# Splitting the output projection's weights early: as extra jobs of the first SwiGLU, kept in DRAM until the attention

## The chip, the cores and the metric

The kernel runs on one core of a Trainium2 chip. The metric is the device time of one execution in microseconds, as the median of several runs. A profile of one execution gives the start, the length and the wait of every instruction on the five engines: TensorE (PE in the profile, its weight loads PEld), VectorE (DVE), ScalarE (ACT), GpSimd (POOL) and SyncE (SP, which here only issues the DMAs).

## The reference, cut to what matters

One transformer block over 1024 tokens of width 1024, in float32:

```python
x = x + 0.5 * swiglu(rms_norm(x, ffn1_norm), ffn1_w_in, ffn1_w_out)      # D_FF = 2816
proj = rms_norm(x, mix_norm) @ w_mix_in                                   # q, k, v, gates
o_a = banded_attention(q_a, k_a, v_a, tbl[:, :8], 128, sinks_a)           # 8 heads, window 128
o_cmp, o_sel = nsa_cmp_sel(q_b, k_c, v_c, k_s, v_s, tbl_b)                # 8 heads, compressed and selected keys
o_win = banded_attention(q_b, k_w, v_w, tbl_b, 512, None)                 # the same 8 heads, window 512
o_b = gates[:, :, 0] * o_cmp + gates[:, :, 1] * o_sel + gates[:, :, 2] * o_win
x = x + concat([o_a, o_b]) @ w_mix_out                                    # the output projection, 1024 x 1024
x = x + 0.5 * swiglu(rms_norm(x, ffn2_norm), ffn2_w_in, ffn2_w_out)
```

## The kernel before, in words

**Arithmetic.** A float32 operand is split in two parts of type fp32r, a high part `h` (the operand rounded) and a low part `l` (what is left). A product is then three matmuls, `h*h + h*l + l*h` (`mm3`, lines 250 to 252). So every weight tile of 128 x 512 that comes from DRAM costs, beside its DMA, one pass that makes `whi` and one subtraction that makes `wlo`.

**Stages.** (1) The first SwiGLU's input stage (`first_stage`) multiplies the normed tokens with `ffn1_w_in`. It uses a Strassen-like scheme of seven products in place of eight for each of 20 pairs of column blocks `n`, so it subtracts weights from each other (line 806) and splits the results on ACT (line 458) and DVE (line 463); on POOL it multiplies gate and up (line 876). Beside this main work it runs *side jobs*: the sums and differences of `ffn1_w_out` that the next stage needs, four loads, four DVE subtractions and four stores to DRAM each (`sums_of`, line 783). A side job works in four fixed buffers: the second halves of the token tiles `X[2]` and `X[3]`, which are free at that time, and two buffers `side`. There are 12 of them, and they follow each other as soon as their buffers come free. (2) `second_stage` multiplies with `ffn1_w_out`. (3) Five chunks of `w_mix_in` make queries, keys, values and gates; the last chunk is called CH1. (4) The attention, in two halves `g` = 0 and 1 of the heads. In each half come eight query tiles `i`, and for each of them three parts A, sel and win: query-key products into PSUM (`lg`, line 1748), a DVE pass that adds the bias and takes the maximum (line 1787), the exponential on ACT (line 1795), its scaling on POOL (line 1811), transposes on PE (`ptr`, line 1923) that ACT and DVE copy out as a high and a low part (`ph` line 1931, `pl` line 1933), the products with the values (`pvo`, lines 1942 and 1943), and a finish on ACT and POOL (lines 1968, 1975, 1981, 1983). After win of tile `i` the output projection of this half follows: four pieces of six matmuls into `mo` (`make_out`), with the eight weight tiles of `w_mix_out` that belong to this half. (5) The second SwiGLU, with both of its stages.

**The weights of the output projection before.** The 16 tiles of 128 x 512 (`MO`, eight for each half) are *converted* in the attention by `conv`: a DMA into one of four buffers `wraw` (line 83), the high part on POOL (`Units.high`, line 88), the low part on DVE (`Units.low`, line 93). The pair `whi`/`wlo` takes one of nine slots. The same nine slots hold the eight tiles of CH1 before, and the scores of the first three attention parts.

**The order of the work.** All instructions are first listed as tasks, each with an engine, an estimated length, a wished position, dependencies and the buffers that it takes. A small planner (`Plan.run`) picks at each step the task that can start earliest by those estimates, and this fixes the program order of every engine. The order is worked out anew when a task is added or removed. On the chip every engine runs its list strictly in that order and waits at an instruction until its inputs are there; SP does the same with the DMAs that it issues, and a DMA also waits until the eighth DMA before it has finished. There are two plans: the first ends with stage 2, and the second holds everything from stage 3 to the end.

Of the kernel before, what the change touches and what calls it, by code (L numbers as in the profile page):

```python
# [9 lines left out]
F32R = mybir.dt.float32r  # L10
BF16 = mybir.dt.bfloat16
I32 = mybir.dt.int32
AF = mybir.ActivationFunctionType
# [7 lines left out]
D = 1024  # L21
KD = 8
FF = 2816
NF = 22
# [15 lines left out]
LATE = 4.5  # L40
# [17 lines left out]
class Units:  # L58
# [7 lines left out]
    def add(self, width, parts):  # L66
        self.units.append((width, parts))
        return len(self.units) - 1
# [120 lines left out]
def block_kernel(  # L189
# [37 lines left out]
    dr = pool("dr", space=DRAM)  # L227
# [26 lines left out]
    def dma(dst, src):  # L254
        if src.dtype == F32R:
            dst, src = dst.bitcast(F32), src.bitcast(F32)
        return nc.sync.dma_start(dst, src)
# [192 lines left out]
    def split(b, dep, src_users, pos, eng, pair=ws.pair, slots=None, chain=None, low="D"):  # L450
# [15 lines left out]
        return w, low, us  # L466

    def acc_ring(turns=("lg", "lg", "lg", "pv", "mo")):
        tile_no[0] += 1
        tag = turns[tile_no[0] % len(turns)]  # L470
        return tag, {"lg": r_lg, "pv": r_pv, "mo": r_mo}[tag]
# [138 lines left out]
    NK = NF // 2  # L610
# [4 lines left out]
    XS = [dr.tile([128, D], F32, name=f"xs{t}") for t in range(NT)]  # L615

    def in_src(w_in, n, j, part):
        return dram_ap(w_in, 512 * j * 2 * FF + part * FF + n * 128, [[4 * 2 * FF, 128], [2 * FF, 4], [1, 128]])
# [8 lines left out]

    def first_stage(layer, w_in, w_out, opn, scaled, units_, side, pos, weigh, at0, pieces, opened, xa=(), raws=None, gain=None, side_free=(), plain=2, begin=False):

# [161 lines left out]
        def weights_of(k):  # L791

            return [lambda j=j, c=c: dram_ap(w_out, (2 * k + j) * 128 * D + c * 512, [[D, 128], [1, 512]])
                    for j in range(2) for c in range(2)]
        SUB, ADD = OP.subtract, OP.add
        T_OPS = (("T1", "T3", "T2", "T4"), TS, ((0, 1, 0, SUB), (1, 3, 1, SUB), (3, 3, 0, SUB), (2, 2, 3, SUB)))
        S_OPS = (("S1", "S3", "S2", "S4"), AS, ((3, 2, 3, ADD), (2, 0, 2, SUB), (0, 3, 0, SUB), (1, 1, 0, SUB)))

        def less(a, b, at, deps):
# [3 lines left out]
            def emit():  # L803
# [10 lines left out]
                                          [stored[0, a] for a in ("A11", "A12", "A21", "A22")], *S_OPS))  # L814
        every = (NF - plain) / (len(jobs) + 0.5)
        half_done = {}
        for n in range(plain, NF):
            while jobs and n - plain >= every * (NK + 1 - len(jobs)):
                side_us = jobs.pop(0)(at)
# [235 lines left out]
    def s2_place():  # L1055
# [3 lines left out]
                                         lambda: side1, 2.0, "G", [],   # L1059
                                              [(0, 256), (256, 512)], none, raws=raws1, gain=lambda c: gcol[:, c], begin=s2_place)  # L1060

# [839 lines left out]
    pvo, mixes, outs = {}, {}, {}  # L1901
    chain = {"pv": None, "mo": None}

    def make_tiles(s):
# [10 lines left out]
        for j, (c, vt) in enumerate(tiles):  # L1915
# [4 lines left out]
            def flip4(c=c, st=st):  # L1920
                p = st["p"] = bank("a", name="ptr")
                for h in range(4):
                    PE.transpose(p[:, h * 128:(h + 1) * 128], s.P[h][:, c:c + 128], ident)  # L1923
            t = add("P", 0.43, pos, flip4, deps=[s.compressed] if vt is None else ready,
                    after=[opened], takes=[(r_a, a_users)])
            s.P_users.append(t)

            def high(st=st):
                st["ph"] = ring(p_kv, "ph", [128, 512], F32R, NPH)
                st["pl"] = ring(p_kv, "pl", [128, 512], F32R, NPH)  # L1930
                ACT.activation(st["ph"], st["p"], AF.Copy)  # L1931
            hi = add("A", 0.48, pos + 0.1, high, deps=[t], takes=[(r_ph, ph_users)])
            lo = add("D", 0.6, pos + 0.2, lambda st=st: DVE.tensor_tensor(  # L1933
# [56 lines left out]
    def make_out(s, parts):  # L1990
        g, i = s.g, s.i
        pos = s.pos + s.nt + 20.0
        for h in range(2):
            box, us, ms = {}, [], []
            for j in range(2):
# [3 lines left out]
                def piece(j=j, h=h, st=st, us_=us_, box=box):  # L1999
                    if j == 0:  # L2000
                        box["o"] = bank("mo")
                    for kk in range(2):
                        wh, wl = ws.out[us_[kk]]
                        mm3(box["o"], st["mh"][:, kk], st["ml"][:, kk], wh, wl, j == 0 and kk == 0, j == 1 and kk == 1)
# [19 lines left out]
    for u, pos in mo_convs:  # L2024
        conv(u, pos, [s.begin for s in subs[:EARLY]])
    for s in subs:
# [92 lines left out]
```

## Time and profile before

| what | us |
|---|---|
| median of 3 runs (lowest, highest) | 1912.22 (1911.73, 1912.34) |
| the profiled execution: its time / its span | 1910.23 / 1908.5 |
| PE busy | 1874.3 (98%) |
| DVE busy | 1373.8 (72%) |
| ACT busy | 920.8 (48%) |
| POOL busy | 428.6 (22%) |

By stage (the stretches are cut by hand at the stages' edges):

| stretch, us | stage | PE | DVE | ACT | POOL | DMA share |
|---|---|---|---|---|---|---|
| 0 to 450 | first SwiGLU, input | 447.0 | 334.2 | 184.6 | 89.0 | 0.51 |
| 450 to 635 | first SwiGLU, output | 185.0 | 110.9 | 84.2 | 0.6 | 0.77 |
| 635 to 880 | projections | 243.8 | 168.2 | 97.7 | 38.6 | 0.41 |
| 880 to 1258 | attention | 354.1 | 328.5 | 304.8 | 225.4 | 0.18 |
| 1258 to 1700 | second SwiGLU, input | 439.6 | 323.9 | 170.2 | 75.1 | 0.49 |
| 1700 to 1908.5 | second SwiGLU, output | 204.7 | 108.1 | 79.4 | 0.0 | 0.64 |

In a row of a timeline stand the start, the length, the engine, the line, the operation with output and inputs, and in brackets the idle time before it with what ended it. In a row of a view by windows stand, for each engine, the busy time and the number of instructions, then the granted TensorE clock, the busy share of the 16 DMA engines and GB/s. "PE 98% busy" counts a matmul that runs at a lower granted clock as busy too.

### The profile page before, as it was taken

Reading aid. Unit: us, or ns where it says so; the run is one execution under the profiler, and the core shown is the slowest. Engines: PE = TensorE matmul, PEld = TensorE weight load, DVE = VectorE, ACT = ScalarE, POOL = GpSimd, SP = SyncE. Lnnn points to the kernel's source line nnn. Section 1 sums busy time; section 2 is a strip of 40 time slices with the busy share of each in tenths; the row PEclk is TensorE's granted clock in tenths of the full one; section 3 lists DMA queues with packets and bytes.
Section 4 is the critical chain, followed back from the end, with each engine's and each line's share of the span. In section 5 each row is a group of like instructions: output and inputs, shape, how many; then the busy total and the mean of one; then the engine's idle time right before and its main releaser. Section 6 shows DMA issues by size and latency. Waiting matters only on the chain.

```text
span 1908.5 us, 27998 instructions
## 1 busy us (share of the span) xinstructions
PE 1874.3 (98%) x9094; PEld 1565.7 (82%) x9094; DVE 1373.8 (72%) x3120; ACT 920.8 (48%) x1951; POOL 428.6 (22%) x568
## 2 busy tenths in 40 slices
PE   9999999999999999998999899999999999999999
PEld 8888888888888889886788788777888888888887
DVE  7978776655755778467988888879788766655553
ACT  6433333333544444346877887854333333344442
POOL 5111111110000112015655764541111111110000
PEclk9999999999999999999999999999999999999999
DMA  5467742327886246244102311023677523368662
GB/s 171 145 225 256 236 153 89 128 97 278 295 252 199 83 118 180 67 141 156 51 23 60 104 61 56 24 66 127 225 232 239 183 92 101 120 238 303 195 214 99
DMA packets 244211, 290.25 MB, mean 152 GB/s; under 512 B 25424, under 2 KB 139488, under 8 KB 244064
## 3 DMA queue, kind: packets, MB, share of 16 engines
q1 hardware_dynamic: 244064, 288.46, 46.4%
q8 instruction: 72, 1.18, 0.3%
q14 instruction: 75, 0.61, 0.1%
HBM read 201.20 MB, written 90.33 MB: 153 GB/s over the span
## 4 chain that ended last, share of the span: by engine, by line
PE 92%; DVE 2%; ACT 2%; POOL 1%; issue 1%; DMA 1%; SPq 0%; DVEq 0%; ACTq 0%
PE lg L250 13%; PE lg L252 13%; PE lg L251 13%; PE mo L250 6%; PE mo L252 6%; PE mo L251 6%; PE pv L250 4%; PE pv L252 4%; PE pv L251 4%; PE ptr L1923 3%; PE a L252 3%; PE a L250 3%; PE a L251 3%; PE pvo L1943 2%; PE lg L1748 2%; PE pvo L1942 2%
## 5 line engine op out<-in xcount | busy, mean ns | idle before, releaser
L876 POOL TENSOR_TENSOR x<-x,x 128x512 f32<-128x512 f32 x80 | 117.6, 1471 | 679.3 <-DVE x L872 640.7
L463 DVE TENSOR_TENSOR wlo<-wraw,whi 128x512 fp32r<-128x512 f32 x286 | 204.3, 719 | 69.2 <-ACT whi L458 68.0
L458 ACT ACTIVATE whi<-wraw 128x512 fp32r<-128x512 f32 x274 | 170.1, 622 | 97.8 <-PE lg L251 46.6
L463 DVE TENSOR_TENSOR gpl<-graw,gph 128x512 fp32r<-128x512 f32 x154 | 106.9, 698 | 124.4 <-ACT gph L458 124.3
L458 ACT ACTIVATE gph<-graw 128x512 fp32r<-128x512 f32 x154 | 96.2, 630 | 195.4 <-PE pv L251 88.5
L868 ACT ACTIVATE x<-lg 128x512 f32<-128x512 f32 x96 | 57.4, 598 | 157.1 <-PE lg L252 157.1
L1933 DVE TENSOR_TENSOR pl<-ptr,ph 128x512 fp32r<-128x512 f32 x178 | 116.4, 684 | 18.3 <-ACT ph L1931 17.1
L1931 ACT ACTIVATE ph<-ptr 128x512 fp32r<-128x512 f32 x178 | 98.5, 595 | 31.1 <-PE ptr L1923 29.4
L88 POOL TENSOR_SCALAR whi<-wraw 128x512 fp32r<-128x512 f32 (+1 forms) x52 | 36.0, 696 | 316.9 <-PE mo L252 209.2
L458 ACT ACTIVATE whi<-x 128x512 fp32r<-128x512 f32 x108 | 67.4, 627 | 81.6 <-PE lg L251 41.6
L250 PE MATMUL a<-whi,gph 128*128 128x512 f32 x264 | 103.1, 391 | 0.0
L252 PE MATMUL a<-whi,gpl 128*128 128x512 f32 x264 | 102.8, 389 | 0.0
L251 PE MATMUL a<-wlo,gph 128*128 128x512 f32 x264 | 102.7, 389 | 0.0
L463 DVE TENSOR_TENSOR wlo<-x,whi 128x512 fp32r<-128x512 f32 x108 | 73.7, 685 | 31.3 <-ACT whi L458 31.1
L250 PE MATMUL lg<-xn0h,whi 128*128 128x512 f32 x232 | 90.7, 391 | 0.0
L252 PE MATMUL lg<-xn0h,wlo 128*128 128x512 f32 x232 | 90.3, 389 | 0.0
L251 PE MATMUL lg<-xn0l,whi 128*128 128x512 f32 x232 | 90.3, 389 | 0.0
L872 DVE TENSOR_TENSOR x<-lg,x 128x512 f32<-128x512 f32 x72 | 49.7, 690 | 54.2 <-PE lg L252 53.9
L252 PE MATMUL lg<-whi,gpl 128*128 128x512 f32 x198 | 77.1, 389 | 0.0
L250 PE MATMUL lg<-whi,gph 128*128 128x512 f32 x198 | 77.0, 389 | 0.0
L251 PE MATMUL lg<-wlo,gph 128*128 128x512 f32 x198 | 77.0, 389 | 0.0
L1811 POOL TENSOR_SCALAR Psel<-Psel,sc,gates 128x256 f32<-128x256 f32 (+7 forms) x60 | 52.1, 871 | 46.1 <-DVE sc L1803 19.8
(523 smaller groups left out, 5698.5 us busy)
## 6 DMA issues: line engine op xcount, KB each, us to landing
wraw<-in_ffn_w_in_dram SPq DMA_DIRECT2D x172, 256.0 KB, 3.3
wraw<-in_ffn_w_out_dram SPq DMA_DIRECT2D x66, 256.0 KB, 3.4
x<-in_ffn_w_out_dram SPq DMA_DIRECT2D x44, 256.0 KB, 4.0
qd<-qst SPq DMA_DIRECT2D x32, 256.0 KB, 2.1
xn0l<-qd SPq DMA_DIRECT2D x32, 256.0 KB, 2.7
wraw<-in_w_mix_in_dram SPq DMA_DIRECT2D x28, 256.0 KB, 2.8
x<-in_x_dram SPq DMA_DIRECT2D x12, 512.0 KB, 6.9
side<-in_ffn_w_out_dram SPq DMA_DIRECT2D x22, 256.0 KB, 4.8
```

Of the source, the lines that this page charges most:

```text
L250: PE.matmul(o, ah, bh, start=first, stop=False, **kw)
L251: PE.matmul(o, ah, bl, start=False, stop=False, **kw)
L252: PE.matmul(o, al, bh, start=False, stop=last, **kw)
L458: ACT.activation(w["h"], b["r"], AF.Copy)
L463: low = add(low, 0.69 if low == "D" else 1.25, pos + 0.5, lambda e=DVE if low == "D" else POOL: e.tensor_tensor(w["l"], b["r"], w["h"].bit ...
L868: ACT.activation(b["r"], o["o"], act)
L872: return add("D", 0.69, at, lambda b=tb[k], o=bx[o]: DVE.tensor_tensor(b["r"], o["o"], b["r"], op=OP.add), deps=deps)
L876: return add("G", 1.25, at, lambda a=tb[a], b=tb[b]: POOL.tensor_tensor(a["r"], a["r"], b["r"], op=OP.mult), deps=deps)
L1811: POOL.tensor_scalar(P[:, off:e], P[:, off:e], sc, gate, op0=OP.mult, op1=OP.mult)
L1923: PE.transpose(p[:, h * 128:(h + 1) * 128], s.P[h][:, c:c + 128], ident)
L1931: ACT.activation(st["ph"], st["p"], AF.Copy)
L1933: lo = add("D", 0.6, pos + 0.2, lambda st=st: DVE.tensor_tensor(st["pl"], st["p"], st["ph"].bitcast(F32), op=OP.subtract), deps=[hi])
```

## The change

The 16 tiles of `w_mix_out` are no longer converted in the attention. Eight more side jobs (`two_aside`) are put behind the twelve of the first SwiGLU's input stage. Each takes two tiles: a load into `X[2]` or `X[3]`, the high part on ACT into a buffer `side`, the low part on DVE in place, and two stores that put both parts in DRAM (`aside`). With 20 jobs in place of 12 the wished positions of the jobs also lie closer together, 0.98 column blocks apart in place of 1.6. In the attention `bring` loads both parts of a tile from DRAM straight into a pair `whi`/`wlo`: two DMAs of 256 KB in place of one, and no work on POOL or DVE. The `wraw` buffers are not used for it, so the second SwiGLU's first weights go into them earlier. Two further dependencies ask that the transposes `ptr` and their copies `ph` are issued in the order in which they are listed. The order of the transposes on PE by their sources (A, sel, win of each tile) is the same in both kernels.

```diff
+    def bring(key, pos, after=()):
+        w, us = {}, []
+        def emit():
+            w["h"], w["l"] = ws.pair()
+            for j, k in enumerate("hl"):
+                dma(w[k], aside[key][j])
+        highs.append(add("S", 0.9, pos, emit, after=[highs[-1], *after], takes=[(r_spl, us)], tail=3.0))
+        return w, highs[-1], us
...
+    aside = {u: dr.tile([2, 128, 512], F32R, name=f"aside{u}") for g in MO for k in g for u in k}
...
+        def two_aside(at, keys):
+            us = [[] for _ in range(4)]
+            for j, key in enumerate(keys):
+                src = ws.units[key][1][0][3]
+                put_ = lambda j, at, key=key: add("S", 0.75, at, lambda: dma(
+                    aside[key][1 - j // 2], side_in()[j].bitcast(F32R)), deps=[us[j][-1]], tail=2.2)
+                t = add("S", 0.75, at, lambda j=j, src=src: dma(side_in()[j], src), takes=[(side_at[j], us[j])], tail=LATE)
+                hi = add("A", 0.6, at + 4.0, lambda j=j: ACT.activation(side_in()[2 + j].bitcast(F32R), side_in()[j], AF.Copy),
+                         deps=[t], takes=[(side_at[2 + j], us[2 + j])])
+                us[2 + j].append(hi)
+                lo = add("D", 0.69, at + 4.5, lambda j=j: DVE.tensor_tensor(
+                    side_in()[j].bitcast(F32R), side_in()[j], side_in()[2 + j], op=SUB), deps=[hi])
...
+                us[2 + j].append(put_(2 + j, at + 6.0))
+                us[j].append(put_(j, at + 6.5))
+            return us
...
-        every = (NF - plain) / (len(jobs) + 0.5)
+        jobs.extend(lambda at, keys=keys: two_aside(at, keys) for keys in ahead)
+        every, n_jobs = (NF - plain) / (len(jobs) + 0.5), len(jobs)
...
-            while jobs and n - plain >= every * (NK + 1 - len(jobs)):
+            while jobs and n - plain >= every * (n_jobs - len(jobs)):
...
-                    after=[opened], takes=[(r_a, a_users)])
+                    after=[opened] + ([chain["fl"]] if chain["fl"] else []), takes=[(r_a, a_users)])
+            chain["fl"] = t
...
-            hi = add("A", 0.48, pos + 0.1, high, deps=[t], takes=[(r_ph, ph_users)])
+            hi = add("A", 0.48, pos + 0.1, high, deps=[t], after=[chain["ph"]] if chain["ph"] else [],
+                     takes=[(r_ph, ph_users)])
+            chain["ph"] = hi
...
     for u, pos in mo_convs:
-        conv(u, pos, [s.begin for s in subs[:EARLY]])
+        ws.out[u], t_, us_ = bring(u, pos, [s.begin for s in subs[:EARLY]])
+        units[u] = t_, us_
```

Three places show how the order moves. The first is on POOL, in the second half of the heads (tile `i` = 1), around the point at which the output projection of the first half is done with its slots. The names are the scores of the three parts (`PA`, `Psel`, `Pwin`) and the output parts (`opart`, `ml`). Before:

```order
L1811 TENSOR_SCALAR Pwin<-Pwin,sc,gates 128x256
L88 TENSOR_SCALAR whi<-wraw 128x512 x4
L1811 TENSOR_SCALAR Pwin<-Pwin,sc,gates 128x256
L1811 TENSOR_SCALAR PA<-PA,sc 128x256 x3
L88 TENSOR_SCALAR whi<-wraw 128x512
L1811 TENSOR_SCALAR PA<-PA,sc 128x256
L88 TENSOR_SCALAR whi<-wraw 128x512
L1811 TENSOR_SCALAR Psel<-Psel,sc,gates 128x384
```

and now (line 1844 is line 1811 of before):

```order
L1844 TENSOR_SCALAR Pwin<-Pwin,sc,gates 128x256 x2
L1844 TENSOR_SCALAR PA<-PA,sc 128x256 x4
L1844 TENSOR_SCALAR Psel<-Psel,sc,gates 128x384 x2
L1865 TENSOR_TENSOR Psel<-Psel,nm 128x4x64
L1844 TENSOR_SCALAR Psel<-Psel,sc,gates 128x384
```

The six conversions are gone, and the scalings follow each other.

The second is on SP at the same point: `qd` are stored queries, `aside_391` to `aside_397` the parts of the second half's tiles (the first of its eight, `aside_390`, comes earlier). Before:

```order
L83 DMA wraw<-in_w_mix_out_dram 128x512
L257 DMA vwin<-vd 128x1024
L257 DMA xn0l<-qd_2_6183 128x512
L257 DMA xn0l<-qd_2_6199 128x512
L257 DMA xn0l<-qd_3_6184 128x512
L257 DMA xn0l<-qd_3_6200 128x512
L83 DMA wraw<-in_w_mix_out_dram 128x512 x2
L257 DMA wraw<-in_ffn_w_in_dram 128x4x128 x4
```

and now:

```order
L257 DMA whi<-aside_392 128x512
L257 DMA wlo<-aside_392 128x512
L257 DMA whi<-aside_393 128x512
L257 DMA wlo<-aside_393 128x512
L257 DMA whi<-aside_394 128x512
L257 DMA wlo<-aside_394 128x512
L257 DMA whi<-aside_395 128x512
L257 DMA wlo<-aside_395 128x512
L257 DMA whi<-aside_396 128x512
L257 DMA wlo<-aside_396 128x512
L257 DMA whi<-aside_397 128x512
L257 DMA wlo<-aside_397 128x512
```

Before, the raw tiles were loaded ahead into the `wraw` buffers and only two loads stood here. Now twelve loads stand in a row, each pair in a slot that the first half's pieces give back. The four query loads stand ahead of them as before, and the next ones after them.

The third is on SP at the start of the attention: `vs` and `vwin` are the values of the first half. Before:

```order
L83 DMA wraw<-in_w_mix_out_dram 128x512 x2
L257 DMA xn0l<-qd_1_6190 128x512
L257 DMA qd_6_6195<-qst 128x512
L83 DMA wraw<-in_w_mix_out_dram 128x512
L257 DMA qd_7_6196<-qst 128x512
L257 DMA vs_8850<-vd 128x1024
L257 DMA vwin<-vd 128x1024
L257 DMA xn0l<-qd_2_6175 128x512
```

and now:

```order
L257 DMA whi<-aside_386 128x512
L257 DMA wlo<-aside_386 128x512
L257 DMA qd_6_6291<-qst 128x512
L257 DMA xn0l<-qd_1_6286 128x512
L257 DMA whi<-aside_387 128x512
L257 DMA wlo<-aside_387 128x512
L257 DMA qd_7_6292<-qst 128x512
L257 DMA whi<-aside_388 128x512
L257 DMA wlo<-aside_388 128x512
L257 DMA xn0l<-qd_2_6271 128x512
L257 DMA vs_8958<-vd 128x1024
L257 DMA vwin<-vd 128x1024
```

Fourteen loads of parts (the first eight stand above this piece) come ahead of `vs`, and the query load `qd_2`, which waits for a buffer that PE gives back, has moved in front of it.

More of the change, by code (lines that the diff above doesn't have):

```diff
@@ L626, in open_in, with first_stage @@
         return t
-    def first_stage(layer, w_in, w_out, opn, scaled, units_, side, pos, weigh, at0, pieces, opened, xa=(), raws=None, gain=None, side_free=(), plain=2, begin=False):
+    def first_stage(layer, w_in, w_out, opn, scaled, units_, side, pos, weigh, at0, pieces, opened, xa=(), raws=None, gain=None, side_free=(), plain=2, begin=False, ahead=()):
         ready = {}
@@ L794, in weights_of @@
                     for j in range(2) for c in range(2)]
+        def two_aside(at, keys):
[10 more added lines that the diff above has]
+                    side_in()[j].bitcast(F32R), side_in()[j], side_in()[2 + j], op=SUB), deps=[hi])
+                us[2 + j].append(lo)
+                us[j].extend([hi, lo])
+                us[2 + j].append(put_(2 + j, at + 6.0))
+                us[j].append(put_(j, at + 6.5))
+            return us
         SUB, ADD = OP.subtract, OP.add
@@ L1059, in block_kernel @@
                                          lambda: side1, 2.0, "G", [],
-                                              [(0, 256), (256, 512)], none, raws=raws1, gain=lambda c: gcol[:, c], begin=s2_place)
+                                              [(0, 256), (256, 512)], none, raws=raws1, gain=lambda c: gcol[:, c], begin=s2_place,
+                                         ahead=[k for g in MO for k in g])
     def to_out():
@@ L1901, in block_kernel @@
     pvo, mixes, outs = {}, {}, {}
-    chain = {"pv": None, "mo": None}
+    chain = {"pv": None, "mo": None, "ph": None, "fl": None}
     def make_tiles(s):
@@ L2002, in piece @@
                     for kk in range(2):
-                        wh, wl = ws.out[us_[kk]]
+                        wh, wl = (ws.out[us_[kk]][k] for k in "hl")
                         mm3(box["o"], st["mh"][:, kk], st["ml"][:, kk], wh, wl, j == 0 and kk == 0, j == 1 and kk == 1)
```

## The prediction

> **What bounds the kernel now.** I read the busy times first, then the busy time in stretches, then the waits of PE in the stretches where PE is idle, then the engine it waits for.
>
> ```profile
> span 1908.5 us, 27998 instructions
> PE 1874.3 (98%) x9094; PEld 1565.7 (82%) x9094; DVE 1373.8 (72%) x3120; ACT 920.8 (48%) x1951; POOL 428.6 (22%) x568
> ```
> ```profile
> 880.00:1258.00 378.00, 354.14 (x2001) 294.76 (x2001) 328.52 (x1300) 304.79 (x789) 225.42 (x379) 0.98 0.18 58
> 880.00:890.00 10.00, 5.46 (x29) 4.71 (x29) 7.98 (x53) 7.70 (x28) 5.40 (x13) 0.74 0.63 210
> 900.00:910.00 10.00, 8.30 (x48) 5.89 (x46) 8.53 (x34) 9.48 (x29) 9.75 (x18) 1.00 0.38 128
> 910.00:920.00 10.00, 8.56 (x43) 5.97 (x41) 9.05 (x43) 8.04 (x24) 6.63 (x15) 1.00 0.19 56
> 920.00:930.00 10.00, 8.09 (x51) 6.58 (x50) 9.40 (x41) 9.41 (x28) 7.99 (x14) 1.00 0.20 55
> 1090.00:1100.00 10.00, 7.02 (x34) 4.48 (x32) 8.56 (x33) 5.95 (x16) 10.00 (x18) 0.99 0.53 157
> 1100.00:1110.00 10.00, 9.92 (x52) 8.30 (x51) 8.43 (x36) 7.85 (x24) 7.12 (x11) 0.84 0.20 54
> ```
>
> PE is the bound: it is idle for only 1908.5 - 1874.3 = 34.2 us, and no matmul is removed. A change that takes nothing from PE can win only idle time, or time at a low granted clock. Of the idle time 378 - 354.1 = 23.9 us lie in the attention, and three places there hold 4.54 (880 to 890), 1.70 + 1.44 + 1.91 = 5.05 (900 to 930) and 2.98 us (1090 to 1100). After two of them the clock is low: 0.74 and 0.84. So the change is worth what it does at these places.
>
> **The change part by part.** It removes from the attention 16 passes on POOL and 16 on DVE:
>
> ```profile
> L88 POOL TENSOR_SCALAR whi<-wraw x16: 607/620/1097, 873.8 to 1095.0; 128x512 fp32r<-128x512 f32 x16
> L93 DVE TENSOR_TENSOR wlo<-wraw,whi x16: 675/706/1092, 876.1 to 1096.1; 128x512 fp32r<-128x512 f32 x16
> ```
>
> That is 16 x 0.62 = 9.9 us of POOL and 16 x 0.71 = 11.3 us of DVE, neither of them the bound. What counts is where they stand in front of something that PE waits for.
>
> *The burst at 1088.* The second half's tiles need the slots of the first half's, so their conversions come all at once when the first half's last pieces are done:
>
> ```profile
> 1087.90 3.24 POOL L88 TENSOR_SCALAR whi<-wraw 128x512 fp32r<-128x512 f32 x4
> 1091.13 1.49 POOL L1811 TENSOR_SCALAR Pwin<-Pwin,sc,gates 128x256 f32<-128x256 f32 x1
> ```
> ```profile
> 1088.87 3.40 DVE L93 TENSOR_TENSOR wlo<-wraw,whi 128x512 fp32r<-128x512 f32 x4
> 1094.93 0.68 DVE L93 TENSOR_TENSOR wlo<-wraw,whi 128x512 fp32r<-128x512 f32 x1
> 1096.15 0.72 DVE L93 TENSOR_TENSOR wlo<-wraw,whi 128x512 fp32r<-128x512 f32 x1
> ```
> ```profile
> 1087.70 0.39 PE L252 MATMUL mo<-whi,ml 128*128 128x512 f32 x1
> ...
> 1092.67 0.77 PE L1923 MATMUL ptr<-ident,Pwin 128*128 128x128 f32 x5 [1.07 <-POOL Pwin L1811]
> ...
> 1097.34 0.44 PE L1748 MATMUL lg<-xn0h,xn0l 128*128 128x384 f32 x1 [0.55 <-DVE nm L1787]
> ...
> 1098.56 0.50 PE L1942 MATMUL pvo<-ph,va 128*128 128x512 f32 x1 [0.60 <-ACT ph L1931]
> ...
> 1100.40 0.80 PE L250 MATMUL mo<-whi,mh 128*128 128x512 f32 x1
> ```
>
> The scaling of `Pwin` ends 1.5 + 3.2 us after the burst began, and PE stands still behind it; ACT and DVE then start late, and the small waits follow. Without the burst this chain has no cause. I take 2.4 of the 2.98 us (from 0, if ACT is as late as before, to 2.98). The slow clock behind it costs (1 - 0.84) x 10 = 1.6 us more, and would go with the gaps: I take 1.4 (0 to 1.6).
>
> By the Trainium skill, page "TensorE: Matmul & The Clock Gate", section "What's actually happening", the clock falls to half after one idle window of about 3.4 us. Here the longest single gap before the fall is 1.07 us, so by that rule the gaps are not its cause and the 1.4 us would not come back; the forecast below would be 4.3 us in place of 5.7. The trace shows the lower clock right behind broken idle time, so I keep the row.
>
> *900 to 930.* Five conversions stand on DVE there:
>
> ```profile
> 900.05 1.29 DVE L93 TENSOR_TENSOR wlo<-wraw,whi 128x512 fp32r<-128x512 f32 x2
> 906.27 0.83 DVE L93 TENSOR_TENSOR wlo<-wraw,whi 128x512 fp32r<-128x512 f32 x1
> 912.17 0.94 DVE L93 TENSOR_TENSOR wlo<-wraw,whi 128x512 fp32r<-128x512 f32 x1
> 915.64 0.68 DVE L93 TENSOR_TENSOR wlo<-wraw,whi 128x512 fp32r<-128x512 f32 x1
> ```
>
> Together 3.74 us, on an engine that is 85 to 94% busy there. ACT is 80 to 95% busy too and gets no relief. So between 0 and 3.7 us of the 5.05 come back; I take half, 1.9.
>
> *880 to 890.* The wait here is for the last tile of the projections to pass through DVE:
>
> ```profile
> 879.04 0.68 DVE L93 TENSOR_TENSOR wlo<-wraw,whi 128x512 fp32r<-128x512 f32 x1
> 880.09 0.49 DVE L1328 CAST kla<-ktr 128x128 fp32r<-128x128 f32 x2 [0.37 <-PE ktr L1317]
> ```
> ```profile
> 883.04 0.36 PE L1748 MATMUL lg<-xn0l 128*128 128x192 f32 x1 [2.72 <-DVE nm L1787]
> ```
>
> DVE was idle for 0.37 us just before, so the conversions that ran ahead of it, the last at 879.04, were already worked off. Little is to be won: 0.5 (0 to 2.7, the whole of the longest wait).
>
> *Added: two loads for one, and later.* Before, the raw tile waited in `wraw`; now both parts are loaded only once the slot is free. Rows for the price:
>
> ```profile
> wraw<-in_w_mix_out_dram SPq DMA_DIRECT2D x16, 256.0 KB, 2.7
> ...
> kd<-kst SPq DMA_DIRECT2D x8, 512.0 KB, 2.9
> x<-in_x_dram SPq DMA_DIRECT2D x12, 512.0 KB, 6.9
> ```
> ```profile
> 450.00:500.00 50.00, 50.00 (x222) 41.40 (x221) 33.48 (x87) 22.37 (x39) 0.56 (x2) 1.00 0.93 326
> ```
>
> A load of 256 KB lands after 2.7 us, and many together pass at up to 326 GB/s, one each 262144 B / 326 GB/s = 0.80 us. At 1088.1 (the end of the matmul at 1087.70) the twelve loads start. The second piece of the new half needs the tenth: 0.3 to issue + 2.7 + 9 x 0.80 = 10.2 us later. PE needs it at 1100.40 - 1088.1 - 2.98 = 9.3 us for the first piece without the gaps, plus some nine more 512-wide matmuls at 0.23 us = 11.4; if 1.5 us of those 9.3 is the slow clock and small gaps, 9.9. So the load is just in time: I add 0.3 us (0 to 3, with 3.7 to land and 0.94 apart at 280 GB/s).
>
> At the start `vs`, 512 KB, now comes behind the query load that waits for PE:
>
> ```profile
> 890.26 1.99 SPq L257 DMA_DIRECT2D xn0l<-qd x2
> ```
> ```profile
> 895.05 0.49 PE L1942 MATMUL pvo<-ph,vs 128*128 128x512 f32 x1
> ```
>
> Issued at about 890.7, it lands at 893.6 (2.9 us) and is needed at 895.05: 0.2 us (0 to 2.5, if it takes the 6.9 us of the crowded loads).
>
> *Added in the first SwiGLU:* 16 passes on ACT, 16 on DVE, 48 DMAs. The last stores of the side jobs of before are issued at 250, so these fall into the quiet part behind:
>
> ```profile
> L257 SPq DMA_DIRECT2D ts_10T<-side x2: 320/320/320, 250.0 to 250.8; - x2
> ```
> ```profile
> 250.00:400.00 150.00, 150.00 (x664) 124.22 (x663) 99.32 (x129) 55.22 (x96) 23.15 (x16) 1.00 0.34 109
> ```
> ```profile
> L463 DVE TENSOR_TENSOR wlo<-wraw,whi 128x512 fp32r<-128x512 f32 x24 | 16.4, 684 | 11.4 <-ACT whi L458 11.4
> L806 DVE TENSOR_TENSOR x<-wraw,x 128x512 f32<-128x512 f32 x9 | 16.0, 1780 | 0.0
> L458 ACT ACTIVATE whi<-wraw 128x512 fp32r<-128x512 f32 x24 | 15.0, 627 | 16.6 <-PE lg L251 8.3 <-PE pv L251 4.2 <-PE mo L251 4.2
> ```
>
> 16 x 0.63 = 10 us on ACT and at most 16 x 1.78 = 28.5 us on DVE (a subtraction that lasts as long as those of line 806) stand against 95 and 51 us of idle time, and ACT's splits wait for PE, not PE for them. The 12.6 MB take 39 us at 326 GB/s out of 150 us in which the DMAs are idle for two thirds. PE was busy all the time there: cost 0, and if this cover were gone, up to 2 us. The twelve older jobs move a little, which this cover hides too. The two dependencies on the transposes leave their order on PE as it was: 0. The rest of the attention is put in another order: 0, from -2 to +3.
>
> **Sum:** -2.4 - 1.4 - 1.9 - 0.5 + 0.3 + 0.2 = -5.7 us. On the profiled execution, 1910.23 us for a span of 1908.5, this gives 1904.5. That execution is 2.0 us below the median of the runs, so against the median I forecast 1912.2 - 5.7 = 1906.5.
>
> **The rivals.** About 0.2%, 3.8 us, is what a measurement of this kernel can tell from no change.
>
> - *All of it comes back.* Both starts run clean: 2.98 + 1.6 + 3.7 + 2.7, and the clock behind 880 to 890, (1 - 0.74) x 10 / 2 = 1.3; 12.3 us, so 1900. For it: DVE is 80% busy or more at all these places. Against it: ACT is up to 95% busy and keeps its work.
> - *The relief goes to ACT's queue.* The waits stay but are named for ACT and for `opart`; only the 1.07 and some of the clock come back: -1.5, 1910.7. For it: the row 900 to 910, where ACT's 9.48 is the longest after POOL's 9.75. Against it: in 1090 to 1100 ACT is only 60% busy.
> - *The loads pass one by one, and it gets slower.* If the twelve loads do not overlap, the tenth lands at 0.3 + 10 x 2.7 = 27.3 us, 16 us after it is needed, and the sum is +10: 1922. It decides in this sense once the loads lie over 2.1 us apart (a stall of 9.8 us). Against it: 326 GB/s of just such loads. The Trainium skill, page "DMA: Bandwidth & Descriptors", section "Bandwidth", has 0.95 us for 64 KB and 6.15 us for 1 MB; a straight line between gives an estimate of 2.0 us for a lone load of 256 KB, about the point at which this rival decides. The 0.80 us of the row speaks against it.
> - *The new order makes new waits.* If each of the 16 tiles of both halves meets one more wait of 0.6 us, as those above, +9.6 - 5.7 = +3.9: 1916. For it: hardly a row of the attention's order on PE is where it was. Against it: between 930 and 1060 PE was almost never idle, and the planner now has less to place.
>
> **How the numbers follow.** My forecast 0.46; all of it 0.12; ACT's queue 0.24; one by one 0.08; new waits 0.10. The forecast's own range is -3 to -9 us (1903 to 1909), mostly beyond 3.8. Faster: 0.46 x 0.85 + 0.12 + 0.03 from the third = 0.54. Slower: 0.08 + half of 0.10 and 0.02 from the unknown order = 0.15. The same: 0.31. The range for 8 in 10 runs from 1899 (all of it) to 1917 (new waits); below it I leave 0.06, above it 0.12.
>
> **What would show it.** Right: no conversion on POOL and DVE in the attention; PE's idle time between 1085 and 1100 under 1 us and the clock behind it at 1.00; 900 to 930 with some 3 us of idle time; 250 to 400 with PE still at 150.00. Wrong: a wait of PE at `mo` for a DMA at the first pieces of the second half, a wait at `pvo` for `vs`, a wait of PE before 400, or idle time of the same size at the same places, named for ACT.

## The result, and the profile after

The changed kernel takes 1899.4 us (median of 4 runs, 1898.5 to 1903.6) against 1912.0 us (1911.6 to 1912.3) of the kernel before: a ratio of 0.9941, 95% interval 0.9928 to 0.9953. It is faster, as forecast, and 1899.4 lies in the range of 1899 to 1917, but at its very edge: the gain is 12.6 us where the sum gave 5.7. That is the size of the first rival. The profiled execution took 1898.5 us for a span of 1896.3, so 12.2 us of span are to be found.

The changed kernel's page, its span and the busy times:

```profile
span 1896.3 us, 28117 instructions
PE 1871.6 (99%) x9094; PEld 1565.6 (83%) x9094; DVE 1371.4 (72%) x3120; ACT 928.8 (49%) x1967; POOL 412.1 (22%) x552
```

Its busy time in stretches, at the places that were shown of the kernel before (length; then busy us of PE, PEld, DVE, ACT, POOL; granted clock, DMA share, GB/s):

```profile
250.00:450.00 200.00, 200.00 (x884) 165.60 (x883) 135.75 (x180) 83.88 (x146) 31.78 (x23) 1.00 0.53 178
880.00:1258.00 378.00, 363.62 (x2061) 305.62 (x2062) 327.09 (x1301) 307.70 (x795) 217.32 (x372) 0.99 0.21 68
880.00:890.00 10.00, 7.28 (x35) 6.62 (x36) 8.63 (x59) 8.98 (x35) 6.17 (x17) 0.68 0.88 306
900.00:910.00 10.00, 9.97 (x55) 8.08 (x56) 9.11 (x42) 9.79 (x31) 8.16 (x18) 1.00 0.19 53
910.00:920.00 10.00, 9.33 (x57) 7.71 (x55) 8.95 (x49) 8.84 (x25) 6.41 (x14) 1.00 0.11 29
920.00:930.00 10.00, 9.55 (x50) 7.24 (x51) 9.59 (x43) 8.62 (x26) 6.29 (x11) 1.00 0.10 26
930.00:940.00 10.00, 8.78 (x49) 6.96 (x47) 8.18 (x35) 9.61 (x25) 8.18 (x15) 1.00 0.08 29
1080.00:1090.00 10.00, 10.00 (x56) 8.70 (x55) 9.21 (x47) 9.74 (x30) 7.99 (x15) 1.00 0.83 283
1090.00:1100.00 10.00, 10.00 (x57) 8.58 (x56) 9.35 (x37) 9.16 (x28) 7.53 (x15) 1.00 0.29 79
1100.00:1110.00 10.00, 9.98 (x61) 8.45 (x60) 8.40 (x35) 8.56 (x25) 5.38 (x13) 1.00 0.13 53
```

Its waits of PE (engine, line, what it waited for: us in all, times, longest):

```profile
PE lg L1781 <- DVE nm L1820: 2.8, 3, 1.8
PE mo L250 <- ACT mh L2017: 2.2, 1, 2.2
...
PE pvo L1979 <- DVE pl L1969: 1.4, 6, 0.3
...
PE pvo L1978 <- ACT opart L2004: 1.2, 3, 0.6
...
PE pvo L1978 <- ACT ph L1965: 0.7, 2, 0.4
```

Three things are to be seen. PE's idle time falls from 34.2 to 24.7 us, and all of that lies in the attention: 23.86 to 14.38 us between 880 and 1258. The second half's start is clean, 10.00 of 10 us busy from 1080 to 1100 at full clock, where 2.98 us were idle and the clock fell to 0.84. And the largest of PE's waits, for `nm`, falls where the forecast had it. The same rows of the kernel before:

```profile
PE lg L1748 <- DVE nm L1787: 5.9, 8, 2.7
PE pvo L1943 <- DVE pl L1933: 3.3, 12, 0.8
PE pvo L1942 <- ACT opart L1968: 3.2, 5, 1.2
PE pvo L1942 <- ACT ph L1931: 2.2, 4, 0.7
```

Of the 5.9 us for `nm`, 5.0 lie between 850 and 950, and 2.4 of the 2.8 us that are left lie there too.

Where the time is won can be worked out from the two profiles without any wait's name. At some matmuls, both kernels have run exactly the same matmuls before, in whatever order; the difference of their start times is the lead of the changed kernel there:

```
start of the matmul before, us     871    950   1089   1103   1117   1299
lead of the changed kernel, us     0.3    5.0    5.3   11.7   12.1   12.1
```

So 4.6 us are won at the start of the attention and 6.4 at the second half's start: 11 of the 12 us lie in the places that the prediction named, and the rest of the attention gives little.

The time lost to a half clock is 6.2 us in the profile before and 6.6 in this one (half of PE's busy time in the lowered stretches), so idle time and clock together explain 9.4 - 0.4 = 9.0 of the 12.2 us. The other 3 us show as busy time of PE. A matmul of 512 columns is shown as 0.39 us while the next one starts after 0.23, so a wait of up to 0.16 us in between is not shown as idle. Behind a wait the rows are shown longer still, as in the kernel before:

```profile
1098.56 0.50 PE L1942 MATMUL pvo<-ph,va 128*128 128x512 f32 x1 [0.60 <-ACT ph L1931]
1099.29 0.50 PE L1943 MATMUL pvo<-pl,va 128*128 128x512 f32 x1 [0.23 <-DVE pl L1933]
```

The second starts 0.73 us after the first, 0.50 more than usual, and only 0.23 of that is shown as idle. Summed over 1088 to 1099.8, the matmuls of the kernel before start 4.76 us later than at the usual distances of their shapes, and 2.98 of it is shown as idle. So 1.8 of the 3 us were waits at the second half's start that the rows show as busy. Where the others went is not shown; profiles with the same order on PE differ by 1.3 us in this remainder.

### The profile page after: what moved, and what is told of

It is laid out like the page before. It is cut to its first block, busy times and chain, and to the rows that moved or that the text cites. A ratio compares the mean times of both kernels' runs of the same rounds, so it can differ in the third digit from the quotient of the medians.

```text
span 1896.3 us, 28117 instructions
## 1 busy us (share of the span) xinstructions
PE 1871.6 (99%) x9094; PEld 1565.6 (83%) x9094; DVE 1371.4 (72%) x3120; ACT 928.8 (49%) x1967; POOL 412.1 (22%) x552
## 4 chain that ended last, share of the span: by engine, by line
PE 93%; DVE 3%; ACT 2%; DMA 1%; issue 1%; SPq 0%; POOL 0%; DVEq 0%; ACTq 0%
PE lg L250 13%; PE lg L252 13%; PE lg L251 13%; PE mo L250 6%; PE mo L251 6%; PE mo L252 6%; PE pv L250 4%; PE pv L252 4%; PE pv L251 4%; PE ptr L1956 3%; PE a L252 3%; PE a L251 3%; PE a L250 3%; PE pvo L1979 2%; PE pvo L1978 2%; PE lg L1781 2%
## 5 line engine op out<-in xcount | busy, mean ns | idle before, releaser
L463 DVE TENSOR_TENSOR wlo<-wraw,whi 128x512 fp32r<-128x512 f32 x286 | 209.9, 739 | 68.2 <-ACT whi L458 67.3
L88 POOL TENSOR_SCALAR whi<-wraw 128x512 fp32r<-128x512 f32 (+1 forms) x36 | 23.3, 651 | 309.5 <-PE mo L252 204.2
```

What stands on the lines that cost most here:

```text
L463: low = add(low, 0.69 if low == "D" else 1.25, pos + 0.5, lambda e=DVE if low == "D" else POOL: e.tensor_tensor(w["l"], b["r"], w["h"].bit ...
```

## The experiments

All ratios are to the kernel before, timed on the same chip; its median was between 1912.0 and 1913.4 us on the chips used. The first theory was the prediction's: the gain is the time that POOL and DVE no longer spend in front of passes that PE waits for ("queues"). The rivals were the order that the planner makes, and the raw slots that come free.

**The order without the work, and the work put back into it.** In the first kernel the planner counts the two conversions of each tile, though nothing is emitted; the next three emit a pass on POOL, on DVE, on both.

```diff
+    held, scratch = [], []
+    fetched.append(add(None, 0.0, 0.0, lambda: scratch.extend(ws.place() for _ in range(2)), after=fetched[-1:],
+                       takes=[(r_raw, held), (r_raw, held)]))
     for u, pos in mo_convs:
         ws.out[u], t_, us_ = bring(u, pos, [s.begin for s in subs[:EARLY]])
         units[u] = t_, us_
+        t = add("G", 0.66, pos, first, deps=[t_, fetched[-1]])         # first: nothing, or a pass of POOL over whi
+        us_.extend([t, add("D", 0.69, pos + 1.0, second, deps=[t])])   # second: nothing, or wlo - whi on DVE
+        held.extend(us_)
```

> The changed kernel, but the planner still reserves 0.66 us on POOL and 0.69 us on DVE for each of the 16 tiles, with nothing emitted in that time; two of the four raw slots are held until the last of them, so that the second SwiGLU's early loads have only two. It tells the order apart from the work. Theory 'queues' (the gain is the time that the conversions no longer take on POOL and DVE in front of passes that PE waits for): as the changed kernel, 1899 us, within 3. Theory 'order' (the gain is the other order that the planner makes once it has nothing to place there): most of it is lost, 1907 to 1912. Theory 'slots' (the gain is raw slots that come free for the second SwiGLU): 1907 to 1912 too, with the loss behind 1100 us.

> As the kernel with reserved time, but in the reserved time POOL really makes one pass of 128x512 over each tile that was loaded, into a raw slot that nothing reads; DVE makes none. PE's matmuls wait for the loads alone. Theory 'queues': POOL's 16 x 0.62 = 9.9 us stand in front of the scalings again; the burst behind 1088 comes back with its slow clock, 2 to 5 us of loss against the kernel with reserved time. Theory 'order': no loss, within 1 us.

> As the kernel with reserved time, but DVE really makes one subtraction of 128x512 from the two loaded parts of each tile, into a raw slot that nothing reads; POOL makes none. Theory 'queues': DVE's 16 x 0.7 = 11.3 us stand in front of the maxima and the low parts again, mostly at 890 to 930; 2 to 5 us of loss against the kernel with reserved time. Theory 'order': no loss, within 1 us.

> As the kernel with reserved time, with both the POOL pass and the DVE pass of each tile made, into raw slots that nothing reads: the engine work of the kernel before, with the loads and the order of the change. Theory 'queues': 5 to 10 us of loss against the kernel with reserved time, at the start and behind 1088, so 1905 to 1910. Theory 'order': no loss, within 1.5 us of it. A loss smaller than the sum of the two single ones means that POOL and DVE delay the same waits.

Measured: nothing emitted 1911.1 us, 0.9995 (0.9985 to 1.0004); POOL's pass 1910.7, 0.9987 (0.9978 to 0.9996); DVE's 1910.9, 0.9991 (0.9982 to 1.0000); both 1913.1, 1.0005 (0.9996 to 1.0014). "Queues" fails at the first of them: POOL and DVE are relieved of all 32 passes, and the whole gain is gone. Nor do the passes cost much when they are put back: some 2 us for both together (the intervals of the two ratios still overlap) where "queues" asked for 5 to 10, and nothing that can be told for one alone.

**The same without the held slots, and the held slots alone.** The first of these reserves as above but leaves the raw slots alone; the second holds two slots until the last load and reserves nothing, so that PE's rows stand exactly as in the changed kernel.

```diff
+    fetched.append(add(None, 0.0, 0.0, ..., takes=[(r_raw, held), (r_raw, held)]))
     for u, pos in mo_convs:
         ws.out[u], t_, us_ = bring(u, pos, [s.begin for s in subs[:EARLY]])
         units[u] = t_, us_
+        held.append(t_)
```

> The kernel with reserved time of the first run (POOL 0.66 and DVE 0.69 us counted by the planner for each tile, nothing emitted), but with no raw slot held. Theory 'order': as that run, 1908 to 1912. Theory 'slots': the gain is back, 1898 to 1901.

> The changed kernel in exactly its own order on PE, with two of the four raw slots held until the last of the 16 loads, as the reserved kernels held them, and nothing else. Theory 'slots' (the gain is raw slots that come free for the second SwiGLU's first loads): the gain goes, 1907 to 1912. Theories 'order' and 'queues': no loss, 1898 to 1901.

Measured: reserved, no slot held: 1911.9 us, 0.9995 (0.9986 to 1.0004). Slots held, nothing reserved: 1900.6, 0.9932 (0.9919 to 0.9945). The slots play no part; the order does. The two reserved kernels, with and without held slots, have the same rows in the same order on PE, ACT, DVE and POOL, so they are one order, timed twice.

How can PE wait more when there is less to do? The timeline of the reserved kernel without held slots, at the second half's start, where no conversion runs (start, length, engine, line, operation; in brackets the idle time before it and what ended it):

```profile
1100.81 1.55 ACT L2004 ACTIVATE opart<-pvo 64x256 f32<-64x256 f32 x4 [2.08 <-PE pvo L1979]
1102.38 0.42 ACT L1869 ACTIVATE Psel<-Psel 128x256 f32<-128x256 f32 x1
1102.83 0.42 DVE L1873 TENSOR_REDUCE den<-Psel 128x4 f32<-128x256 f32 x1 [3.15 <-ACT Psel L1869]
...
1104.22 0.34 DVE L1818 TENSOR_SCALAR_CACHE_REDUCE Pwin<-lg,mx 128x128 f32<-128x128 f32 x1
...
1104.68 0.36 PE L1781 MATMUL lg<-ka,xn0l 128*128 128x256 f32 x1 [1.96 <-issue]
```
```profile
1105.00:1110.00 5.00, 4.75 (x16) 3.68 (x15) 4.86 (x17) 2.92 (x9) 2.72 (x5) 0.66 0.00 2
```

ACT stands 2.08 us at the copies of `pvo`; DVE's next row, the sum of `Psel`, needs ACT's row behind those copies, so DVE stands 3.15 us; the maxima of `Pwin`, which would free a bank of `lg`, are queued behind that sum, and PE stands 1.96 us. (The view has "issue" for PE's wait; that the bank is what it waits for is read from the DVE row that ends just before.) The clock falls to 0.66 behind it. Each queue runs strictly in the order written, and this order was written for engines that are busy at other times.

The lead of this kernel over the kernel before, worked out as above, shows where its gain goes:

```
start of the matmul before, us     871    950   1089   1103   1114   1299
lead of the reserved kernel, us   -1.3   -1.4   -2.0    4.4    0.2   -1.3
```

Without the burst of conversions it wins the same 6.4 us between 1089 and 1103 as the changed kernel, and loses 4.2 of them again within 12 us, at the wait just shown and the slow clock behind it. At the start of the attention it wins nothing: PE is idle for 0.8 us less up to 944, but 3.6 us more are lost to the half clock. Of the 13.9 us between the spans of this kernel (1910.2) and the changed one, 7.7 are idle time and 4.7 are half clock (11.3 us lost to it against 6.6).

**The work without room for it.** Two kernels make the reverse test. In the first, PE's rows stand exactly as in the changed kernel, and the two passes are emitted but counted as 0. In the second, the kernel before keeps all its conversions and has no side jobs, and the planner counts them as 0.

```diff
+        t = add("G", 0.0, pos, lambda w=ws.out[u]: POOL.tensor_scalar(scratch[0]..., w["h"]..., 1.0, 1.0, ...), deps=[t_, ...])
+        us_.extend([t, add("D", 0.0, pos + 1.0, lambda w=ws.out[u]: DVE.tensor_tensor(scratch[1]..., ...), deps=[t])])
```
```diff
-        highs.append(add("G", 0.66, pos, lambda: ws.high(u), deps=fetched[-1:], ...
+        highs.append(add("G", 0.0 if u in MOS else 0.66, pos, lambda: ws.high(u), deps=fetched[-1:], ...
-        low = add("D", 0.69, pos + 1.0, lambda: ws.low(u), deps=highs[-1:])
+        low = add("D", 0.0 if u in MOS else 0.69, pos + 1.0, lambda: ws.low(u), deps=highs[-1:])
```

> The changed kernel with PE's and ACT's rows in exactly the order of the change, but POOL makes one pass of 128x512 and DVE one subtraction for each of the 16 loaded tiles, into raw slots that nothing reads; the planner is told that they cost nothing, so that they don't move anything. Theory 'queues' (the gain is the freed time of POOL and DVE): the gain goes, 1907 to 1912. Theory 'order' (the gain is where the rows stand once the planner no longer places the conversions): the gain stays, 1898 to 1902; and the first four runs say that 16 passes cost some 1 to 2 us in an order that has room for them.

> The kernel before with all its conversions in the attention and no side jobs, but the planner is told that the 16 conversions cost nothing on POOL and DVE (and has the two chains, without which it finds no order): an order close to that of the change (164 of PE's rows elsewhere), with the work of the kernel before at its own places. Theory 'match': no gain, or a loss, 1909 to 1916, since the work stands where the order has no room for it. Theory 'order alone': 1899 to 1904.

Measured: 1910.2 us, 0.9990 (0.9981 to 0.9999), and 1907.6, 0.9974 (0.9965 to 0.9983). So the very passes that cost 2 us in the reserved order (1913.1 against 1911.1) cost about 10 in the changed kernel's (1910.2 against 1900.6 with the same slots held). By what was written before, the first of these runs speaks for "queues" and against "order", as the reserved kernels spoke the other way: each of the two theories fails on one of the tests. The timeline of the first of the two shows its longest wait of PE:

```profile
904.25 5.42 DVE L2067 TENSOR_TENSOR wraw<-wlo,whi 128x512 fp32r<-128x512 f32 x6
909.58 0.42 DVE L1820 CUSTOM_DVE_ANT_0 Pwin<-lg,xn0h 128x256 f32<-128x256 f32 x1
```
```profile
910.06 0.58 PE L1781 MATMUL lg<-xn0h,xn0l 128*128 128x256 f32 x1 [4.40 <-DVE nm L1820]
```

Six passes stand one behind the other in front of the maxima, since the planner, told that they cost nothing, did not spread them. (This profiled execution took 1913.7 us, 3.5 more than the median of its kernel, and 4.5 us of its distance to the changed kernel's profile arise ahead of the attention. So the 10 us are told by the medians alone.) The second kernel, with the conversions at their own places, has it on POOL at the second half's start, four conversions of 3.25 us in front of `Pwin`, as the kernel before had:

```profile
1086.85 3.25 POOL L88 TENSOR_SCALAR whi<-wraw 128x512 fp32r<-128x512 f32 x4
1090.09 1.49 POOL L1813 TENSOR_SCALAR Pwin<-Pwin,sc,gates 128x256 f32<-128x256 f32 x1
```
```profile
1091.64 0.42 PE L1925 MATMUL ptr<-ident,Pwin 128*128 128x128 f32 x1 [3.33 <-POOL Pwin L1813]
```

It is still 4.5 us faster than the kernel before, so about a third of the gain is to be had by this order alone, with all the work in place. Neither of the pure theories foresaw that: "match", as I had written it, gave no gain or a loss, and "order alone" the whole of it.

**The added work alone.** All eight side jobs, but the attention converts as before, with PE's rows exactly as before:

```diff
-        ws.out[u], t_, us_ = bring(u, pos, [s.begin for s in subs[:EARLY]])
-        units[u] = t_, us_
+        conv(u, pos, [s.begin for s in subs[:EARLY]])
```

> The eight added side jobs of the change in the first SwiGLU, with all their loads, splits and stores, but the attention converts the 16 tiles as the kernel before did and in the order of the kernel before on PE; what the jobs stored is not read. It prices the added work by itself. All theories: hidden behind PE, 1911 to 1913, no wait of PE before 450 us that was not there. A rival (the added work costs and hides part of the gain): over 1914.

Measured: 1912.2 us, 1.0003 (0.9994 to 1.0012). Its stretch where the jobs run:

```profile
250.00:450.00 200.00, 200.00 (x884) 165.62 (x883) 136.07 (x180) 83.48 (x146) 32.14 (x23) 1.00 0.53 178
```

PE is busy for all of it. The added work costs nothing that can be measured.

**Another order without the work.** If the gain were one lucky order, another would lose it.

```diff
-        highs.append(add("S", 0.9, pos, emit, after=[highs[-1], *after], takes=[(r_spl, us)], tail=3.0))
+        highs.append(add("S", 0.9, pos, emit, after=[highs[-1], *after], takes=[(r_spl, us)], tail=4.4))
```

> The changed kernel with one number of the planner changed: it takes a load of the split tiles to land after 4.4 us in place of 3.0 (4.2 to 4.6 were measured). No work is added or taken; some 380 of PE's rows stand elsewhere. Theory 'match' (formed after the eight runs before: the gain needs the conversions gone and an order made without them, and any order made for the work that is really there keeps it): 1897 to 1903. Theory 'luck' (the order of the change is one lucky draw among many, and another order without conversions loses as the reserved one did): 1904 to 1912.

Measured: 1898.3 us, 0.9926 (0.9914 to 0.9938). With some 380 rows of PE elsewhere the gain is kept. Together:

```
                                     planner counts the conversions   planner does not count them
the conversions (or passes) run      1912.0 (before), 1913.1          1910.2, 1907.6
nothing runs                         1911.1, 1911.9                   1899.4 (changed), 1900.6, 1898.3
```

Taking the work away gives nothing while the order still makes room for it. Leaving the room away gives 2 to 4.5 us while the work is still there (the 2 are barely clear of no change). The two together give 12.6. Two different orders without the conversions are equally fast, one that reserves time loses the gain with and without held slots. What was not tried: other orders that reserve the time. So it stays open whether a better order for the kernel before exists, and whether the reserved order is a typical one or a bad draw.

**Filling PE's waits.** The clock in these profiles is lowered in pieces of 3.41 us, 6.83 and 10.24, at starts that lie whole multiples of 3.41 us apart. The changed kernel's busy time in that raster (columns as above; PE's busy time is the second number):

```profile
880.19:883.60 3.41, 1.19 (x7) 0.88 (x8) 3.31 (x22) 3.38 (x11) 1.39 (x3) 1.00 1.05 356
883.60:890.43 6.83, 6.52 (x31) 6.12 (x32) 5.50 (x41) 5.47 (x25) 5.21 (x16) 0.50 0.81 284
1238.60:1242.01 3.41, 1.47 (x11) 1.20 (x9) 2.80 (x6) 2.80 (x7) 1.41 (x3) 1.00 0.00 0
1242.01:1245.43 3.42, 3.20 (x8) 2.12 (x9) 2.77 (x4) 1.21 (x3) 3.05 (x3) 0.50 0.00 0
1276.15:1279.57 3.42, 1.24 (x4) 0.84 (x5) 3.42 (x5) 2.80 (x6) 2.00 (x2) 1.00 0.00 0
1279.57:1282.98 3.41, 3.41 (x9) 2.68 (x9) 3.41 (x4) 0.68 (x2) 2.78 (x2) 0.50 0.00 0
```

Each lowered piece follows a window in which PE was busy for 35 to 43%. To test that this is the cause, matmuls that nothing reads were put in front of the longest waits:

```diff
+    def fill(o, n):
+        for _ in range(n):
+            PE.matmul(o[:, :128], identr, identr, start=True, stop=True, skip_group_check=True)
...
+                n_fill = {1: 13, 2: 4}.get(pieces[0][0], 0) if s is subs[1] else 0      # first selected heads
+                if n_fill:
+                    fill(bank("pv", name="fill"), n_fill)
...
+                    elif h == 0 and s is subs[-1]:                                      # last output piece
+                        fill(bank("lg", name="fill"), 18)
...
+                                if there:                                               # second SwiGLU, second token half
+                                    fill(o["o"], 18)
```

> The changed kernel with four groups of matmuls of 128x128 that nothing reads, put in front of the four longest waits of PE: 13 and 4 at the first selected heads (waits of 1.78 and 0.66 us), 18 before the last head's output piece (2.16 us), 18 before the second SwiGLU's first product of its second half (0.49 + 1.89 us). They do no work; they keep PE busy while it waits. Theory 'window' (the clock is halved for 3.41 us after each 3.41 us in which PE was busy for less than about half): the half-clock windows at 883 (6.83 us), 1242 and 1279 go, and with them up to 6.57 us; 1893 to 1897. Theory 'gap' (it is the gaps' sum, or something other than PE's busy share, that halves the clock) : no gain, 1899 to 1901, or a loss if the groups last longer than the waits.

Measured: 1897.4 us, 0.9925 (0.9913 to 0.9938), 0.4 us above the range of the window theory and below that of the other. The same stretches of the filled kernel:

```profile
1238.60:1242.01 3.41, 3.39 (x29) 3.16 (x27) 2.79 (x6) 2.84 (x7) 1.38 (x2) 1.00 0.02 5
1242.01:1245.43 3.42, 2.86 (x16) 2.27 (x17) 3.37 (x6) 1.18 (x3) 3.21 (x4) 1.00 0.00 0
1276.15:1279.57 3.42, 2.76 (x16) 2.19 (x15) 3.42 (x5) 1.83 (x4) 1.52 (x2) 1.00 0.00 0
1279.57:1282.98 3.41, 3.41 (x16) 2.82 (x16) 3.41 (x4) 1.61 (x4) 2.84 (x2) 1.00 0.00 0
```

The clock stays at 1.00 behind both waits, and the time lost to it falls from 6.6 to 1.7 us. The raster of this execution lies 0.2 us later, so what each fill did has to be read there: without the unread matmuls PE would be busy for 36% of the window in front of 1242, with them for 94%, so this is a test. The two windows in front of 1280 would be at 59 and 69% without them, and might have kept the clock in any case; there the next kernel is the test, where the window that ends at 1278 is at 39% without and 81% with them, and the clock stays up. The span falls by less, 2.6 us: at 938, when the third sum of the output projection is added to `x`, the filled kernel stands just 0.1 us ahead of the changed one, though 1.6 of the 3.3 us that the clock took at the start are back. That PE waits there for other engines in any case is the likely reason, not shown. The time against the changed kernel is not told apart by the intervals (0.9925 and 0.9941). So the fills show that keeping PE busy in a window keeps the clock up behind it; that they shorten the kernel is not shown.

**Both together.** The loads counted as 4.4 us, and the fills:

> The changed kernel with both edits of the last two runs that were as fast as it or faster: loads counted as 4.4 us by the planner, and the four groups of unread matmuls in front of PE's longest waits. If the half clock costs time only where PE is what sets the end (behind 1242 and 1279), two windows of 3.41 us, 2 x 1.7 us, are to be had against the kernel that has only the other order, less what was hidden by waits: 1895 to 1897.5, 0.991 to 0.9925 of the kernel before. If the groups gave nothing: 1898.3, as that kernel.

Measured: 1895.8 us (1913.4 before, on the same chip), 0.9912 (0.9896 to 0.9929). It is the fastest of all medians, faster than the kernel before by 0.7 to 1.0%; against the changed kernel the intervals just touch (0.9928 there, 0.9929 here), so that last step is likely, not shown. The clock still took 3.4 us of its profiled execution, all at the start of the attention.

## Why the prediction was right or wrong

*The places were right, the sizes were not, and one step was missing.* The direction, the two places and the range hold, but the sum gave 5.7 us and 12.6 came. By the lead above the second half's start gave 6.4 us where the sum had 2.4 + 1.4 = 3.8, and the start of the attention 4.6 where it had 1.9 + 0.5 = 2.4. "A change that takes nothing from PE can win only idle time, or time at a low granted clock" set the bound too low: 1.8 us of waits at 1088 stood in PE's busy time.

The missing step is the order. The prediction priced the removed passes by what stands behind them in the old order, and set "the rest of the attention is put in another order: 0". In the reserved order the same removal gives 0.3 us in all (1911.9 against 1912.2): the 6.4 us of the burst come there too, and new waits with their slow clock take them back. So what the removal is worth is not fixed before the order is known, and the zero was a price for one favourable order. That the measured time still lies in the range, at its edge, is in part luck: the planner's new order made few new waits, which nothing in the prediction had shown.

*The burst at 1088*, -2.4 forecast: the 2.98 us of idle time are gone, the upper bound, and with them the 1.8 us that the rows hid. But the reserved kernel, which has no burst either, stood 1.96 us at about the same place, so "without the burst this chain has no cause" was too strong: another order gave PE another wait just behind it.

*The slow clock at 1100*, -1.4: 1.6 us came back there (1.00 for 0.84). But another lowered piece stands at 1279 now, so in all the clock gave nothing back (6.2 us lost before, 6.6 after). The row was kept against the rule that the prediction cites, and rightly so: the window in front of 1100 had no gap over 0.6 us and was busy for 60%, and the fills then showed such a cause at another wait. By the rule the sum would have been -4.3, farther off.

*900 to 930*, -1.9: 5.05 us idle became 0.03 + 0.67 + 0.45, but 1.22 us stand at 930 to 940, where PE was not idle before: -2.7 in all. The row of the kernel before:

```profile
930.00:940.00 10.00, 10.00 (x55) 8.38 (x54) 8.39 (x38) 6.88 (x18) 4.26 (x10) 1.00 0.07 27
```

"Some 3 us of idle time" in 900 to 930 was forecast, 1.15 were found.

*880 to 890*, -0.5: the idle time went from 4.54 to 2.72 us, and the clock fell a little further, from 0.74 to 0.68. The reason given for a small gain, that the conversions were worked off by then, did not settle it: 1.8 us of the idle time went.

*Later loads*, +0.3 and +0.2: no wait of PE names a load, so no cost of theirs is seen. Twelve loads in a row at 1088 were assumed; in the new order they are issued from 1077.2 on, as the slots come free one by one. Their rows:

```profile
1077.23 0.43 SPq L257 DMA_DIRECT2D whi<-aside  x1
...
1086.57 0.43 SPq L257 DMA_DIRECT2D wlo<-aside  x1
```
```profile
whi<-aside SPq DMA_DIRECT2D x16, 256.0 KB, 4.2
wlo<-aside SPq DMA_DIRECT2D x16, 256.0 KB, 4.6
```

They took 4.2 and 4.6 us (medians) to land where 2.7 was assumed for the first, and it did not matter.

*The first SwiGLU*, 0: right, and priced by itself (1.0003). *The two chains*, 0: built into the kernel before they leave every row of every engine where it was, so 0 for them alone is right; but without them the planner finds no order at all for the changed attention, so they are part of what makes the new order possible.

*The rivals.* "All of it comes back", 1900 at a chance of 0.12, is the result in its size, though not in its terms: 2.72 us of the idle time at 880 to 890 stayed, and the clock gave nothing back in all. It was held back because ACT keeps its work, yet the waits for `opart` and `ph`, both ACT's, fell as well (3.2 to 1.2 and 2.2 to 0.7 us) without ACT doing less in the attention. "The relief goes to ACT's queue" had a chance of 0.24 and is refuted by the same numbers. "The loads one by one" did not happen. "The new order makes new waits" had the right subject, the order; it is not what the changed kernel's order did, and it is what the reserved order did.

## What to carry to other kernels

Where a planner writes the order of the queues, the work that is removed and the time that the planner reserves for it are two changes, and each may be worth nothing without the other: run the kernel once with the time reserved and nothing emitted, and once with the work emitted and nothing reserved. Here this was seen with one reserved order and two free ones. Price a moved order by the idle time and the slow clock that waits of PE make in that stage, as a range from 0 to all of it, not as 0, and remember that a wait can also stand in rows that are shown as busy: compare the distances of the matmuls' starts. To see where a moved order wins or loses, compare the start times of matmuls before which both kernels have done the same work. And where PE must wait anyway for half a window, a few matmuls that nothing reads kept the clock up here; a gain in time by them alone was not clear of the noise.

## What the runs showed of the hardware

The clock is lowered after windows of 3.41 us with a small busy share of PE, not by one long gap alone: in front of 1100 in the kernel before, no gap in the window is over 0.6 us. All windows at full clock between 20 and 1880 us of the fourteen profiled executions, sorted by PE's busy share in them, worked out from PE's rows and the clock's records:

```
PE busy in a window of 3.41 us     followed by half clock     not followed by it
under 45%                          33                         0
45 to 55%                           6                         6
55 to 65%                           5                        18
65 to 80%                           2                        72
over 80%                            0                      7403
```

Each lowered window costs up to 1.7 us, and where the raster happens to lie decides too: the changed kernel and the one with held slots have the same rows on PE, and had four and two of them. The Trainium skill, page "TensorE: Matmul & The Clock Gate", section "What's actually happening", has the window of 3413 ns that runs freely, and the trace agrees; it has half the clock "after ≥1 idle window", and here it came after windows that were up to 62% busy. The measurement decides. The two cases over 65% (71 and 78%) are both at the start of the filled kernels' attention, in windows that hold many short matmuls, and of 12 windows at 45 to 55% only half were followed by the half clock. Busy time is not the whole measure, and what else counts stays open.

A half clock need not cost its time: at the start of the filled kernel's attention 1.6 us came back as clock, and 0.1 as time.
